# A second head group's chunk states and state products as float32r triples, with gate columns kept in DRAM and decays computed in place

## The chip, the cores and the metric

The kernel runs on one core of a Trainium2 chip. A time is the device time of one execution in microseconds (us). A core has five instruction streams that run side by side and wait for each other by semaphores: TensorE (PE, matrix products), VectorE (DVE), ScalarE (ACT), GpSimd (POOL) and SyncE (SP, which here only issues DMAs). "PEld" in the profile is PE's loading of the stationary operand, which overlaps its products. POOL issues a few DMAs too.

## The reference

One block of a decoder over 1024 positions of width 1024, all in float32. Two kinds of mixer share one input projection and one output projection; a squared-ReLU MLP follows.

```python
u = rms_norm(h, g_mix) * (1 + scale_m) + shift_m
proj = u @ w_in                                   # columns: pool | z | xBC | dt
y_pool = pool_mixer(proj[pool], w_pool, pool_scale)   # windows 2, 4, 8, 16
y_ssd = ssd_mixer(z, u_xbc, u_dt, ...)
h = h + gate_m * (concat(y_pool, y_ssd) @ w_out)
h = h + gate_f * (relu(u2 @ w_up)**2 @ w_down)        # u2: norm of h again
return rms_norm(h, g_final)
```

The state-space mixer (SSD) has 2 groups of 8 heads, 64 wide, with a state of 128, and goes over 8 chunks of 128 positions. Of it:

```python
scores = einsum('bclgn,bcsgn->bclsg', cc, bc)               # C times B inside a chunk
y_diag = einsum('bclsgr,bcsgrp->bclgrp', scores * decay_in, xdt)
states = einsum('bclgn,bclgr,bclgrp->bcgrpn', bc, decay_out, xdt)    # chunk states
# scan over the chunks: h * dec + st, each chunk gets the state ahead of it
y_off = einsum('bclgn,bcgrpn,bclgr->bclgrp', cc, prev, exp(a_cum))   # C times state
y = (y_diag + y_off + d_skip * xs) * silu(z)
```

The products of a chunk's B with the decayed inputs (chunk states) and of its C with the running state are the ones that the change touches; and, of `silu(z)`, the first 240 of the 1024 gate columns.

## The kernel before

Large products run as three float32r products of high and low parts (`mm3`): a float32 operand is cast to float32r on ACT (the high part), DVE subtracts that from the operand (the low part), and PE adds high × high, high × low and low × high in one PSUM bank. Each is a row of line 247 in the profile. The small products of the SSD are plain float32 matmuls. They are shown as two records each (x2, "passes").

The program runs in this order:

1. Startup, then projections for x, B and C of head group 0, with the causal convolution behind each (to about 245 us, with group 1's projections in their second half). Among them, `z0_tok` computes the first 240 gate columns and the dt columns for each of 8 row tiles: ACT takes tanh into `zt` (2 buffers), and DVE writes the sum into `z0s`, a tile of 128x8x240 that stays in SBUF until the SSD of group 0 multiplies it into `tok`.
2. `queue_ssd(g)` puts 9 items in the list `side`: item c calls `ssd_a(c)` (scores; decays: ACT takes exp of a row `R` into `dec`, DVE multiplies by the scores; `ssd_x` makes `xdt` on DVE and `xw` on POOL; B is turned and copied to `btok`), then `ssd_r(c+1)` (loads the next `R` from `cum_d` and masks it on POOL), then `ssd_b(c-1)`. In `ssd_b`, PE forms C × state into bank `po` (line 743), the 8 products of the decayed scores with `xdt` into `py` (L746), and `btok` × `xw` into `pst_` (L750). POOL then multiplies the state by the chunk's decay (L756), DVE adds `pst_` (L757), adds `py` to `tok` (L758), scales `po` (L761) and adds that (L763).
3. `step()` sits between projections and takes items from `side`. Group 0's items run between group 1's projections (to about 230 us); group 1's run in the pool mixer's stage, one per half of a window group (`pool_half`, L797 to L823, about 240 to 300 us, with `pp` the difference that PE multiplies by `wp` at L821), and the last three between the first 512 gate columns' tiles t = 0, 1, 2 in `z_tok` (300 to 318 us).
4. At t = ZC (3) the pool `mx`, which held all SSD tiles, is closed; its space goes to the pools `late` and `fslots`. `gm` and `gf` (512 KB each, L958 and L959) are loaded there, ada columns are computed on DVE from weights in the ring `raw` of 4 buffers (`ada_chunk`, `acc`, L852 for the first and L854 for the rest), and `z_weights` (L917) loads the second half of the gate weights through the same ring. The ring also serves reloads of `ypool_d` and, by `unit` (L193 to L199), the output projection's weights.
5. Output projection, then the MLP, to the end at 1150 us.

The order on each engine is that of a scheduler which lays the program out ahead of time; tiles with fewer buffers than uses make a writer wait for the readers of the buffer's last use. `rows of SP` below are DMAs in the order in which the one queue takes them: one that waits holds back all behind it.

Of the kernel before, what the change touches and what calls it, by code (L numbers as in the profile page):

```python
# [27 lines left out]
HD = 64  # L28
# [22 lines left out]
Z0 = 240  # L51
# [21 lines left out]
def tile_hybrid_block(  # L73
# [24 lines left out]
    pe, act, dve, pool, sp = nc.tensor, nc.scalar, nc.vector, nc.gpsimd, nc.sync  # L98
# [141 lines left out]
    def mm3(ps, whi, wlo, a, first, last, weights_first=True, more=False):  # L240
        ahi, alo = a
        if weights_first:
            three = ((whi, ahi), (whi, alo), (wlo, ahi))
        else:
            three = ((ahi, whi), (ahi, wlo), (alo, whi))
        for i, (st_, mv) in enumerate(three):
            pe.matmul(ps, lhsT=st_, rhs=mv, start=first and i == 0, stop=last and i == 2, skip_group_check=more)  # L247
# [293 lines left out]
    mx = ExitStack()  # L541
    mp = enter(mx, name="mix", bufs=1)
    carry = {ct: mp.tile([P, 4], F32, name=f"carry{ct}") for _, ct in G0}
    z0s = mp.tile([P, NT, Z0], F32, name="z0s")
    dtr = mp.tile([P, NT, HEADS], F32, name="dtr")
    da = mp.tile([P, NT, HEADS], F32, name="da")
    ncum = mp.tile([P, P], F32, name="ncum")
# [4 lines left out]
    BC = {}  # L552
# [42 lines left out]
    def z0_tok(t, ks):  # L595
        ps = bank()
        tok_mm(ps[:, :256], t, ks)
        dve.tensor_tensor(out=dtr[:, t, :], in0=ps[:, Z0:256], in1=dtb, op=ALU.add)
        th = accp.tile([P, 272], F32, name="zt", tag="zt", bufs=2)
        act.activation(out=th[:, :Z0], in_=ps[:, :Z0], func=AF.Tanh, scale=0.5)  # L600
        dve.scalar_tensor_tensor(out=z0s[:, t, :], in0=th[:, :Z0], scalar=1.0, in1=ps[:, :Z0],
                                 op0=ALU.add, op1=ALU.mult)

    def feat(ks, h):
        ps = bank()
# [31 lines left out]
    conv_half(G1[0][1], 1, feat(ks1, 1))  # L637
    step(5.2)

    ax, e_, s_, cumt = (mp.tile([P, HW], F32, name="dec", tag="dec", bufs=4)[:, :P] for _ in range(4))  # L640
    xf = dtr.rearrange("p t h -> p (t h)")
    daf = da.rearrange("p t h -> p (t h)")
    tc.keep_in_program_order(act.activation(out=nea, in_=nea, func=AF.Exp))
# [43 lines left out]

    def ssd_r(g, c_):
        a = c_ * HEADS + g * 8
        R = mp.tile([P, 8, P], F32, name="R", tag="R", bufs=2)  # L690
        sp.dma_start(out=R.rearrange("p h l -> p (h l)"),
                     in_=cum_d[a // 8:a // 8 + 1, :].broadcast_to([P, S]))
        pool.affine_select(out=R, in_=R, pattern=[[0, 8], [1, P]], compare_op=ALU.is_ge, fill=-1e38, base=0,
                           channel_multiplier=-1)
        Rs[(g, c_)] = R

# [14 lines left out]
    def ssd_a(g, c_):  # L711
        B, C = BC[8 + g], BC[10 + g]
        cs = slice(c_ * P, (c_ + 1) * P)
        pscore = bank()
        pe.matmul(pscore[:, :P], lhsT=B[:, cs], rhs=C[:, cs], start=True, stop=True)
        sc = pscore[:, :P]
        Ms = []
        R = Rs.pop((g, c_))
        for b in range(2):
            dec = mp.tile([P, HW], F32, name="dec", tag="dec", bufs=4)  # L720
            dv = dec.rearrange("p (h l) -> p h l", l=P)
            for i in range(4):
                a = c_ * HEADS + g * 8 + b * 4 + i
                act.activation(out=dv[:, i, :], in_=R[:, 4 * b + i, :], func=AF.Exp, bias=ncum[:, a:a + 1])
            dve.tensor_tensor(out=dv, in0=dv, in1=sc.unsqueeze(1).broadcast_to([P, 4, P]), op=ALU.mult)
            Ms.append(dec)
        xdt, xw = ssd_x(g, c_)
        btok = None
        if c_ < NT - 1:
            pb = bank()  # L730
            turn(pb[:, :P], B[:, cs])
            btok = mp.tile([P, P], F32, name="btok", tag="btok", bufs=2)
            act.copy(btok, pb[:, :P])
        live[(g, c_)] = (Ms, xdt, xw, btok)

    def ssd_b(g, c_):
        Ms, xdt, xw, btok = live.pop((g, c_))
        C = BC[10 + g]
        cs = slice(c_ * P, (c_ + 1) * P)
        yv = tok[:, c_, g * 512:(g + 1) * 512]  # L740
        if c_ > 0:
            po = bank()
            pe.matmul(po, lhsT=C[:, cs], rhs=states[g], start=True, stop=True)  # L743
        py = bank()
        for hh in range(8):
            pe.matmul(py[:, hh * HD:(hh + 1) * HD], lhsT=Ms[hh // 4][:, (hh % 4) * P:(hh % 4 + 1) * P],  # L746
                      rhs=xdt[:, hh * HD:(hh + 1) * HD], start=True, stop=True)
        if c_ < NT - 1:
            pst_ = bank()
            pe.matmul(pst_, lhsT=btok, rhs=xw, start=True, stop=True)  # L750
            if c_ == 0:
                states[g] = mp.tile([P, HW], F32, name="state", tag="state", bufs=1)
                act.copy(states[g], pst_)
            else:
                sv = states[g].rearrange("p (h d) -> p h d", d=HD)
                pool.tensor_tensor(out=sv, in0=sv, in1=hbc(cdec, c_, g, HD), op=ALU.mult)  # L756
                dve.tensor_tensor(out=states[g], in0=states[g], in1=pst_, op=ALU.add)  # L757
        dve.tensor_tensor(out=yv, in0=yv, in1=py, op=ALU.add)  # L758
        if c_ > 0:
            y1 = mp.tile([P, HW], F32, name="y1", tag="y1", bufs=1)  # L760
            dve.tensor_tensor(out=y1.rearrange("p (h d) -> p h d", d=HD),  # L761
                              in0=po.rearrange("p (h d) -> p h d", d=HD), in1=hbc(ea, c_, g, HD), op=ALU.mult)
            dve.tensor_tensor(out=yv, in0=yv, in1=y1, op=ALU.add)  # L763
        if g == 0:
            dve.scalar_tensor_tensor(out=tok[:, c_, 0:Z0], in0=tok[:, c_, 0:Z0], scalar=0.5, in1=z0s[:, c_, :],
                                     op0=ALU.mult, op1=ALU.mult)

    def queue_ssd(g):
        ssd_r(g, 0)
        for c_ in range(NT):  # L770
            def one(c_=c_):
                ssd_a(g, c_)
                if c_ + 1 < NT:
                    ssd_r(g, c_ + 1)
                if c_ > 0:
# [776 lines left out]
    for p in range(7):  # L1552
# [6 lines left out]
        ps = sets[key]  # L1559
# [78 lines left out]
```

## Time and profile before

| what | us |
|---|---|
| runs, median of 3 | 1150.16 (1148.13 to 1151.42) |
| profiled execution, its own time | 1152.16 |
| span of the profile | 1150.5 |
| PE busy | 1138.3 (99%) |
| DVE busy | 822.2 (71%) |
| ACT busy | 562.6 (49%) |
| POOL busy | 148.2 (13%) |
| L743, C × state, in 247 to 320 us | 14 records, 7.2 |
| L750, chunk states, there | 14 records, 7.5 |

The granted PE clock was 0.997 of full speed. Busy time is a sum over the span and says little about a stage; the chain that ended last, followed back from the last instruction, says what set the end in each. In the rows of the trace the first number is the start in us from the span's beginning, the second the length; a bracket at the end holds the time that the engine stood idle before it, and what it waited for.

### The profile page before, as it was taken

What the parts mean: (1) busy time and instruction counts of PE and PEld (TensorE: products, weight loads), DVE (VectorE), ACT (ScalarE), POOL (GpSimd) and SP (SyncE); (2) the same over time, 40 slices, a digit from 0 to 9 for tenths busy, and PEclk for the clock granted to TensorE, in tenths of its full rate; (3) what the DMA queues carried; (4) which work ended last, traced back from release to release, by engine and by line L of the source; (5) the groups of instructions that cost most, each with busy time, mean ns of one, the idle gap of its engine ahead of it and who ended that gap; (6) DMA issues with size and microseconds to landing.
All of it is one profiled execution on the core that took longest, in us unless ns stands there. A gap on an engine that the chain in (4) does not pass through costs nothing.

```text
span 1150.5 us, 15234 instructions
## 1 busy us (share of the span) xinstructions
PE 1138.3 (99%) x5541; PEld 948.1 (82%) x5541; DVE 822.2 (71%) x1230; ACT 562.6 (49%) x985; POOL 148.2 (13%) x188
## 2 busy tenths in 40 slices
PE   9999999999999999999999999999999999999997
PEld 9889887877898888888788888888888888888886
DVE  4769989967878667666987666665458744586985
ACT  4477575544354424545774444444434344434373
POOL 3011335425400012022000000000100000000030
PEclk9999999999999999999999999999999999999999
DMA  9932432223256656863165434342599835775832
GB/s 280 254 114 64 131 92 83 93 86 115 74 183 188 226 191 229 257 198 114 36 238 192 174 134 168 143 160 88 211 382 345 308 94 162 254 238 196 279 116 90
DMA packets 123899, 200.72 MB, mean 174 GB/s; under 512 B 8464, under 2 KB 65584, under 8 KB 121776
## 3 DMA queue, kind: packets, MB, share of 16 engines
q1 hardware_dynamic: 122464, 196.24, 50.9%
q0 software_dynamic: 1120, 3.21, 0.9%
q8 instruction: 43, 0.70, 0.3%
q10 hardware_dynamic: 240, 0.30, 0.1%
q14 instruction: 32, 0.26, 0.1%
HBM read 159.81 MB, written 39.91 MB: 174 GB/s over the span
## 4 chain that ended last, share of the span: by engine, by line
PE 79%; DVE 7%; DMA 7%; ACT 2%; issue 2%; POOL 1%; POOLq 0%; SPq 0%; DVEq 0%; ACTq 0%
PE bank L247 70%; DMA raw<-in_w_ada_dram 4%; PE bank L746 2%; DVE acc L854 2%; DMA raw<-ypool_d 1%; DMA raw<-in_w_out_dram 1%; DVE lo L199 1%; PE bank L141 1%; PE bank L750 1%; PE bank L338 1%; PE bank L743 1%; PE bank L821 1%; POOL rst L183 1%; POOL tok L1001 0%; DVE wx L1179 0%
## 5 line engine op out<-in xcount | busy, mean ns | idle before, releaser
L247 PE MATMUL bank<-u,hi 128*128 128x512 f32 x560 | 182.6, 405 | 0.5 <-ACT u L390 0.4
L247 PE MATMUL bank<-dlo,dhi 128*128 128x512 f32 (+1 forms) x464 | 177.2, 382 | 0.0
L247 PE MATMUL bank<-dhi 128*128 128x512 f32 (+1 forms) x464 | 177.2, 382 | 0.0
L247 PE MATMUL bank<-dhi,dlo 128*128 128x512 f32 (+1 forms) x464 | 177.1, 382 | 0.0
L1457 ACT CAST dhi<-fr 128x1024 fp32r<-128x1024 f32 x56 | 58.9, 1052 | 142.8 <-PE bank L247 109.1
L247 PEld LDWEIGHTS bank<-u,hi 128*128 128x128 f32 x560 | 103.7, 189 | 26.6 <-issue 4.8
L1458 DVE TENSOR_TENSOR dlo<-fr,dhi 128x1024 fp32r<-128x1024 f32 x56 | 68.4, 1222 | 78.6 <-ACT dhi L1457 77.9
L247 PE MATMUL bank<-hi,ym 128*128 128x512 f32 x384 | 123.6, 395 | 0.0
L247 PE MATMUL bank<-u,lo 128*128 128x512 f32 x280 | 110.2, 393 | 0.0
L198 ACT CAST hi<-raw 128x512 fp32r<-128x512 f32 (+2 forms) x101 | 62.9, 634 | 80.2 <-DMA raw<-in_w_out_dram 41.6
L247 PEld LDWEIGHTS bank<-dlo,dhi 128*128 128x128 f32 x464 | 87.2, 188 | 17.0
L247 PEld LDWEIGHTS bank<-dhi,dlo 128*128 128x128 f32 x464 | 87.2, 188 | 17.0
L247 PEld LDWEIGHTS bank<-dhi 128*128 128x128 f32 x464 | 87.2, 188 | 16.8
L199 DVE TENSOR_TENSOR lo<-raw,hi 128x512 fp32r<-128x512 f32 (+2 forms) x101 | 75.1, 752 | 30.3 <-ACT hi L198 29.9
L247 PE MATMUL bank<-E,whl 128*128 128x512 f32 x384 | 92.7, 391 | 0.1
L247 PEld LDWEIGHTS bank<-E,whl 128*128 128x128 f32 x384 | 71.7, 188 | 16.6 <-DVE whl L1231 0.9
L247 PEld LDWEIGHTS bank<-hi,ym 128*128 128x128 f32 x384 | 72.1, 188 | 14.8 <-ACT hi L198 0.2
L183 POOL TENSOR_TENSOR rst<-ssq,mhalf 128x1 f32<-128x1 f32 (+2 forms) x27 | 26.5, 984 | 401.7 <-DVE ssq L182 368.2
L247 PE MATMUL bank<-u,whl 128*128 128x512 f32 x312 | 75.6, 389 | 0.0
L247 PE MATMUL bank<-lo,ym 128*128 128x512 f32 x192 | 74.9, 390 | 0.2 <-DVE lo L199 0.2
L247 PEld LDWEIGHTS bank<-u,whl 128*128 128x128 f32 x312 | 58.5, 188 | 12.5 <-DVE whl L1231 0.5
L1231 DVE TENSOR_TENSOR whl<-wraw,whl 128x512 fp32r<-128x512 f32 x58 | 39.9, 688 | 38.4 <-ACT whl L1226 38.3
(272 smaller groups left out, 2144.9 us busy)
## 6 DMA issues: line engine op xcount, KB each, us to landing
f_d<-tok SPq DMA_DIRECT2D x16, 1792.0 KB, 7.1
wr<-in_w_down_dram SPq DMA_DIRECT2D x56, 512.0 KB, 5.6
fr<-f_d SPq DMA_DIRECT2D x53, 512.0 KB, 4.8
raw<-in_w_ada_dram SPq DMA_DIRECT2D x64, 256.0 KB, 2.9
wraw<-in_w_up_dram SPq DMA_DIRECT2D x15, 1024.0 KB, 5.3
raw<-in_w_in_dram SPq DMA_DIRECT2D x48, 256.0 KB, 3.1
raw<-in_w_out_dram SPq DMA_DIRECT2D x48, 256.0 KB, 3.1
tok<-in_x_dram SPq DMA_DIRECT2D x16, 512.0 KB, 6.4
```

Source lines behind the costliest of these rows:

```text
L141: return pe.transpose(dst, src, ident)
L183: pool.tensor_tensor(out=rst[:, a:b], in0=m, in1=mhalf[:, :b - a], op=ALU.pow)
L198: act.copy(hi[:, :n], raw[:, :n])
L199: dve.tensor_tensor(out=lo[:, :n], in0=raw[:, :n], in1=hi[:, :n].bitcast(F32), op=ALU.subtract)
L247: pe.matmul(ps, lhsT=st_, rhs=mv, start=first and i == 0, stop=last and i == 2, skip_group_check=more)
L338: pe.matmul(warm_ps[:, 0:P], lhsT=ones, rhs=ones, start=True, stop=True)
L743: pe.matmul(po, lhsT=C[:, cs], rhs=states[g], start=True, stop=True)
L746: pe.matmul(py[:, hh * HD:(hh + 1) * HD], lhsT=Ms[hh // 4][:, (hh % 4) * P:(hh % 4 + 1) * P], rhs=xdt[:, hh * HD:(hh + 1) * HD], start=Tru ...
L854: dve.scalar_tensor_tensor(out=acc[0], in0=raw, scalar=cact[:, k:k + 1], in1=acc[0], op0=ALU.mult, op1=ALU.add)
L1231: dve.tensor_tensor(out=t_[:, 1], in0=src, in1=t_[:, 0].bitcast(F32), op=ALU.subtract)
L1457: act.copy(hi, src)
L1458: dve.tensor_tensor(out=lo, in0=src, in1=hi.bitcast(F32), op=ALU.subtract)
```

## The change

It has three parts.

For head group 1 only, the chunk-state product and C × state become `mm3` triples. For that, `two_parts` makes high and low parts of the state (`shl`), of `xw` (`xhl`), of `btok` (`bhl`) and of the chunk's C (`chl`), each by a cast on ACT and a subtraction on DVE. Group 0 keeps its float32 matmuls.

The gate columns no longer stay in SBUF: the sum is made in `zt`, stored to `z0_d` by a DMA on POOL's queue (120 KB a tile), and loaded again by SP into a tile `z0` of two buffers, one item ahead of its use.

Decays are computed in place: ACT writes exp over `R`, DVE multiplies there, and the 8 products read it. The tag `dec` with its 4 buffers is gone, `R` has 3 buffers and not 2, and the scratch tiles of the dt block lie in one of them.

```diff
@@ z0_tok
-        dve.scalar_tensor_tensor(out=z0s[:, t, :], in0=th[:, :Z0], scalar=1.0, in1=ps[:, :Z0],
+        dve.scalar_tensor_tensor(out=th[:, :Z0], in0=th[:, :Z0], scalar=1.0, in1=ps[:, :Z0],
                                  op0=ALU.add, op1=ALU.mult)
+        pool.dma_start(out=z0_d[t], in_=th[:, :Z0])
@@ dt block
-    ax, e_, s_, cumt = (mp.tile([P, HW], F32, name="dec", tag="dec", bufs=4)[:, :P] for _ in range(4))
+    dts = mp.tile([P, 8, P], F32, name="R", tag="R", bufs=3)
+    ax, e_, s_, cumt = (dts[:, i, :] for i in range(4))
@@ ssd_r
-        R = mp.tile([P, 8, P], F32, name="R", tag="R", bufs=2)
+        R = mp.tile([P, 8, P], F32, name="R", tag="R", bufs=3)
@@ ssd_a
-            dec = mp.tile([P, HW], F32, name="dec", tag="dec", bufs=4)
-            dv = dec.rearrange("p (h l) -> p h l", l=P)
+            dv = R[:, 4 * b:4 * b + 4, :]
...
-                act.activation(out=dv[:, i, :], in_=R[:, 4 * b + i, :], func=AF.Exp, bias=ncum[:, a:a + 1])
+                act.activation(out=dv[:, i, :], in_=dv[:, i, :], func=AF.Exp, bias=ncum[:, a:a + 1])
...
-            Ms.append(dec)
+            Ms += [dv[:, i, :] for i in range(4)]
@@ new
+    def low_part(v, src):
+        dve.tensor_tensor(out=v[:, 1, :], in0=src, in1=v[:, 0, :].bitcast(F32), op=ALU.subtract)
+
+    def two_parts(name, src, n=HW):
+        v = mp.tile([P, 2, n], F32R, name=name, tag=name, bufs=1)
+        act.copy(v[:, 0, :], src)
+        low_part(v, src)
+        return v
@@ ssd_b
-            pe.matmul(po, lhsT=C[:, cs], rhs=states[g], start=True, stop=True)
+            if g == 0:
+                pe.matmul(po, lhsT=BC[10][:, c_ * P:(c_ + 1) * P], rhs=states[g], start=True, stop=True)
+            else:
+                shl, chl = shls[g], chls.pop((g, c_))
+                mm3(po, shl[:, 0, :], shl[:, 1, :], (chl[:, 0, :], chl[:, 1, :]), True, True, False)
...
-            pe.matmul(pst_, lhsT=btok, rhs=xw, start=True, stop=True)
+            if g == 0:
+                pe.matmul(pst_, lhsT=btok, rhs=xw, start=True, stop=True)
+            else:
+                xp, bp = xhl.pop((g, c_))
+                mm3(pst_, xp[:, 0, :], xp[:, 1, :], (bp[:, 0, :], bp[:, 1, :]), True, True, False)
...
+            if g:
+                shls[g] = two_parts("shl", states[g])
...
-            dve.scalar_tensor_tensor(out=tok[:, c_, 0:Z0], in0=tok[:, c_, 0:Z0], scalar=0.5, in1=z0s[:, c_, :],
+            dve.scalar_tensor_tensor(out=tok[:, c_, 0:Z0], in0=tok[:, c_, 0:Z0], scalar=0.5, in1=z0r.pop(c_),
                                      op0=ALU.mult, op1=ALU.mult)
@@ queue_ssd, in an item
+                if g == 0:
+                    z0r[c_] = mp.tile([P, Z0], F32, name="z0", tag="z0", bufs=2)
+                    sp.dma_start(out=z0r[c_], in_=z0_d[c_])
                 if c_ > 0:
                     ssd_b(g, c_ - 1)
+                if g and c_ < NT - 1:
+                    xhl[(g, c_)] = two_parts("xhl", live[(g, c_)][2]), two_parts("bhl", live[(g, c_)][3], P)
+                if g and c_ > 0:
+                    chls[(g, c_)] = two_parts("chl", BC[10 + g][:, c_ * P:(c_ + 1) * P], P)
```

The changed file's lines are shifted against those of the profile: L743 and L750 of before stand at L248 (`mm3`, L247 before), L746 at L762, L757 at L777, L758 at L780, L761 at L783, L763 at L785, L725 at L730, L852 at L881, L917 at L946, L958 and L959 at L987 and L988.

In the pool stage the triples stand where the float32 matmuls stood. On PE in the z stage, at the item that runs after tile t = 0, before:

```order
L715 MATMUL bank<-ct,bt 128x128
L141 MATMUL bank<-ident,bt 128x128
L743 MATMUL bank<-state,ct 128x512
L746 MATMUL bank<-xdt,dec 128x64 x8
L750 MATMUL bank<-xw,btok 128x512
L247 MATMUL bank<-hi,u 128x272
```

and now, where `hi,u` and `lo,u` are the products of the next tile's gate columns:

```order
L248 MATMUL bank<-shl,chl 128x512
L762 MATMUL bank<-xdt,R 128x64 x8
L248 MATMUL bank<-shl,chl 128x512
L248 MATMUL bank<-xhl,bhl 128x512
...
L248 MATMUL bank<-xhl,bhl 128x512
L248 MATMUL bank<-lo,u 128x272
...
L248 MATMUL bank<-xhl,bhl 128x512
L248 MATMUL bank<-shl,chl 128x512
L248 MATMUL bank<-hi,u 128x272 x2
```

The scheduler took the triples apart: the second product of C × state stands behind the eight products with the decays, and the third one and two of the chunk state's among the next tile's products.

On DVE the first ada product (`acc`) stood in the pool stage, behind the step's last sum, before:

```order
L701 TENSOR_TENSOR xdt<-tok,dt 128x512
L763 TENSOR_TENSOR tok<-tok,y_2953 128x512
L852 TENSOR_SCALAR acc<-raw,cact 128x512
L804 TENSOR_TENSOR psum<-craw 128x527
L725 TENSOR_TENSOR dec<-dec,bank 128x512
```

and stands in the last step of the z stage now, with the low parts in the steps before it:

```order
L777 TENSOR_TENSOR state<-state,bank 128x512
L780 TENSOR_TENSOR tok<-tok,bank 128x512
L783 TENSOR_TENSOR y_3408<-bank,ea 128x512
L742 TENSOR_TENSOR shl<-state,shl 128x512
L785 TENSOR_TENSOR tok<-tok,y_3408 128x512
L742 TENSOR_TENSOR chl<-ct,chl 128x128
...
L939 SCALAR_TENSOR_TENSOR tok<-tok,zt 128x272
L783 TENSOR_TENSOR y_3459<-bank,ea 128x512
L881 TENSOR_SCALAR acc<-raw,cact 128x512
L785 TENSOR_TENSOR tok<-tok,y_3459 128x512
```

The low part of the state is the third operation after the state's sum, and `acc` has moved by about three steps, to right ahead of the last sum of the SSD.

On SP's queue at the same place, before:

```order
L917 DMA raw<-in_w_in_dram 128x512
L816 DMA wp<-in_w_pool_dram 128x128
L823 DMA ypool_d<-yo 128x512
L691 DMA R<-cum_d 128x1024
L823 DMA ypool_d<-yo 128x512 x2
L958 DMA gm<-in_b_ada_dram 128x1024
L959 DMA gf<-in_b_ada_dram 128x1024
```

and now:

```order
L852 DMA ypool_d<-yo 128x512
L946 DMA raw<-in_w_in_dram 128x512
L987 DMA gm<-in_b_ada_dram 128x1024
L988 DMA gf<-in_b_ada_dram 128x1024
L875 DMA raw<-in_w_ada_dram 128x512
L946 DMA raw<-in_w_in_dram 128x512 x2
```

The fourth load of z weights, which takes the buffer that `acc` frees, has moved from ahead of the last pool-stage loads to right ahead of `gm` and `gf`.

More of the change, by code (lines that the diff above doesn't have):

```diff
@@ L133, in tile_hybrid_block @@
     ypool_d = dramp.tile([4, P, S], F32, name="ypool_d")
+    z0_d = [dramp.tile([P, Z0], F32, name=f"z0_d{t}") for t in range(NT)]
     hres_d = [dramp.tile([P, D], F32, name=f"hres{t}") for t in range(NT)]
@@ L543, in tile_hybrid_block @@
     carry = {ct: mp.tile([P, 4], F32, name=f"carry{ct}") for _, ct in G0}
-    z0s = mp.tile([P, NT, Z0], F32, name="z0s")
     dtr = mp.tile([P, NT, HEADS], F32, name="dtr")
@@ L680, in tile_hybrid_block @@
     states = {}
+    shls = {}
+    z0r = {}
+    xhl = {}
+    chls = {}
     def hbc(t, c_, g, n):
@@ L734, in ssd_a @@
         live[(g, c_)] = (Ms, xdt, xw, btok)
+    def low_part(v, src):
[5 more added lines that the diff above has]
+        return v
     def ssd_b(g, c_):
         Ms, xdt, xw, btok = live.pop((g, c_))
-        C = BC[10 + g]
-        cs = slice(c_ * P, (c_ + 1) * P)
         yv = tok[:, c_, g * 512:(g + 1) * 512]
@@ L742, in ssd_b @@
             po = bank()
-            pe.matmul(po, lhsT=C[:, cs], rhs=states[g], start=True, stop=True)
+            if g == 0:
[3 more added lines that the diff above has]
+                mm3(po, shl[:, 0, :], shl[:, 1, :], (chl[:, 0, :], chl[:, 1, :]), True, True, False)
         py = bank()
         for hh in range(8):
-            pe.matmul(py[:, hh * HD:(hh + 1) * HD], lhsT=Ms[hh // 4][:, (hh % 4) * P:(hh % 4 + 1) * P],
+            pe.matmul(py[:, hh * HD:(hh + 1) * HD], lhsT=Ms[hh],
                       rhs=xdt[:, hh * HD:(hh + 1) * HD], start=True, stop=True)
```

## The prediction

> **What bounds the kernel now.** I read the page's busy shares first, then the chain that ended last, then the waits in the stretch where that chain leaves TensorE (PE).
>
> ```profile
> PE 1138.3 (99%) x5541; PEld 948.1 (82%) x5541; DVE 822.2 (71%) x1230; ACT 562.6 (49%) x985; POOL 148.2 (13%) x188
> ...
> PE 79%; DVE 7%; DMA 7%; ACT 2%; issue 2%; POOL 1%; POOLq 0%; SPq 0%; DVEq 0%; ACTq 0%
> ```
>
> PE is busy for 99% of the span, yet the chain gives it only 79%. The difference lies in one stretch, as the chain's own rows in order of time show:
>
> ```profile
> 301.29 0.86 PE bank L743 x2
> ...
> 303.88 0.91 PE bank L750 x2
> ...
> 317.96 6.04 PE bank L247 x48
> ...
> 329.06 4.11 DMA raw<-in_w_ada_dram
> ...
> 336.87 3.53 DMA raw<-in_w_ada_dram
> ...
> 461.25 6.57 DMA raw<-in_w_out_dram
> ...
> 468.50 0.70 DVE lo L199
> ...
> 469.24 2.79 PE bank L247 x11
> ...
> 586.32 552.85 PE bank L247 x2470
> ```
>
> Up to 324 us (317.96 + 6.04) PE sets the end. From 329 to 469 us the chain runs through loads into the four `raw` buffers, each waiting for VectorE (DVE) or ScalarE (ACT) to free one. PE works there too, but meets that ring just in time, at 469.24. Then PE sets the end again: 2470 matmuls without a gap from 586 us. A microsecond that PE wins before 324 us therefore reaches the end only if the ring also starts a microsecond earlier. All edits lie before 320 us. The second group's stage, 247 to 320 us, cut at its steps:
>
> ```profile
> 263.00:273.00 10.00, 10.00 (x50) 7.75 (x49) 8.49 (x14) 4.66 (x13) 6.62 (x7) 1.00 0.26 88
> ...
> 284.00:294.00 10.00, 10.00 (x50) 7.62 (x50) 8.16 (x15) 3.88 (x11) 5.89 (x5) 1.00 0.27 98
> 294.00:304.00 10.00, 10.00 (x70) 8.53 (x69) 10.00 (x16) 4.82 (x16) 5.12 (x4) 1.00 0.07 26
> 304.00:312.00 8.00, 8.00 (x51) 6.33 (x49) 6.20 (x11) 3.94 (x12) 4.56 (x4) 1.00 0.21 68
> 312.00:320.00 8.00, 8.00 (x61) 7.31 (x60) 5.67 (x11) 2.67 (x6) 0.00 (x0) 1.00 0.29 98
> sum 73.00, PE 73.00 PEld 58.28 DVE 56.78 ACT 31.90 POOL 30.19; mean PE 10.43 PEld 8.33 DVE 8.11 ACT 4.56 POOL 4.31
> ```
>
> The columns are the stretch, its length, then busy time of PE, weight loads, DVE, ACT and POOL. PE is full everywhere. DVE has 16.2 us free over 73, but 1.5 and 1.8 us in a pool step and none from 294 to 304.
>
> **The change part by part.**
>
> *Products.* Seven C×state and seven chunk-state matmuls cost 0.86 and 0.91 us (chain rows above). A float32r triple of that size is what the projections run; the first products of two triples, six triples apart:
>
> ```profile
> 220.64 0.62 PE L247 MATMUL bank<-u,hi 128*128 128x512 f32 x2
> ...
> 224.74 0.62 PE L247 MATMUL bank<-u,hi 128*128 128x512 f32 x2
> ```
>
> 4.10 / 6 = 0.68 us, or 0.23 a product. Saved: 7 × 0.18 + 7 × 0.23 = 2.9 us, taken as it stands, since the same shapes run in both rows. "FP8 and Floating Point Precision" of the Trainium skill (TensorE Precision Notes) says that true FP32 takes four passes; that would be 0.91 us for both kinds and a saving of 14 × 0.23 = 3.2 us. The 0.86 us of the C×state row is a little below it, so I use the rows.
>
> *Splitting the operands.* For each of seven chunks ACT casts and DVE subtracts: state and x·w (512 wide), B and C (128 wide).
>
> ```profile
> 305.50 0.68 DVE L758 TENSOR_TENSOR tok<-tok,bank 128x512 f32<-128x512 f32 x1
> 306.10 0.69 DVE L761 TENSOR_TENSOR y<-bank,ea 128x512 f32<-128x512 f32 x1
> ```
>
> ```profile
> L908 DVE SCALAR_TENSOR_TENSOR zt<-zt,bank 128x272 f32<-128x272 f32 x3 | 1.3, 432 | 1.4 <-ACT zt L907 1.3
> L919 ACT CAST zw<-raw 128x512 fp32r<-128x512 f32 x3 | 1.6, 611 | 0.0
> L733 ACT COPY btok<-bank 128x128 f32<-128x128 f32 x7 | 1.8, 258 | 0.0
> ```
>
> DVE: 14 × 0.60 (the pace of the two rows) + 14 × 0.25 (128 wide; below 0.43 for 272, and 0.60 × 128/512 = 0.15 is the floor) = 11.9 us, 1.7 per step. ACT: 14 × 0.61 + 14 × 0.26 = 12.2 us, against 41 us free: no cost by itself. The state's cast and subtraction lengthen the recurrence: state add, cast, subtraction, product. The state add and the product that needs it:
>
> ```profile
> 304.90 0.69 DVE L757 TENSOR_TENSOR state<-state,bank 128x512 f32<-128x512 f32 x1 [0.73 <-PE bank L750]
> ...
> 308.70 1.02 PE L743 MATMUL bank<-state,ct 128*128 128x512 f32 x2
> ```
>
> From 305.59 to 308.70 there are 3.1 us. The triple's first product needs only the cast: 2.5 us are left. Its later products stand behind eight matmuls. From 294 to 304 DVE has no room for its 1.7 us, so it runs that late: 0.8 us are left. By the order DVE also has `y` ahead of `shl`, and `y` waits for the split triple's last product, some products later. I take 0.7 us of stall for the three steps of the z stage, between 0 and 1.4 (twice).
>
> *The first low part.* At 240 us DVE now has `xhl` between the two short corrections of `pp`, for which PE waits:
>
> ```profile
> 239.42 0.16 DVE L813 TENSOR_TENSOR pp<-pp,craw 128x1 f32<-128x1 f32 x1
> ...
> 240.37 1.02 PE L821 MATMUL bank<-pp,wp 128*128 128x512 f32 x2
> ```
>
> 0.8 us separate them. A subtraction of 0.60 fits; one of 1.5 (below) doesn't, by 0.7. I take 0.3. PE at 320 us is then 2.9 − 0.7 − 0.3 = 1.9 us earlier, between 0.8 and 2.9.
>
> *Gate columns.* Eight 120 KB stores on POOL's queue and eight reloads on SP's. The tanh result stays in one of two `zt` buffers until its store lands, and ACT and what is behind it (weight casts, convolution) waits for that. Nearest rows: the POOL queue's 512 KB loads, and the stretch itself.
>
> ```profile
> fr<-f_d POOLq DMA_DIRECT2D x3, 512.0 KB, 9.2
> ```
>
> ```profile
> 60.00:110.00 50.00, 49.70 (x326) 45.15 (x325) 40.27 (x76) 37.23 (x68) 8.63 (x23) 1.00 0.25 69
> ```
>
> At most 9.2 us for a buffer, at least a quarter of it, 2.3. ACT has 12.8 us free and PE is fed from weights cast ahead; I take 0, with up to 2 us in the range. The issues stand on POOL ahead of the convolution's `craw` and `carry` copies. The reloads have tens of microseconds before their use, behind `cum_d` rows on SP: 0. DVE's work is the same in count.
>
> *Decays in place, three R slots.* No instruction is added. A row of decays no longer waits for a `dec` slot, and its cast of the next chunk can begin earlier; R's next load waits for PE's last use instead of ACT's. With three slots that is two steps back: 0.
>
> *Loads at the end of the stage.* On SP the fourth z-weight load now stands right ahead of `gm` and `gf`, and waits for the first ada product on DVE, which has moved into the z stage. So 1 MB that was issued at 310 us, into idle queues, comes at about 318, ahead of the ring's own loads.
>
> ```profile
> gm<-in_b_ada_dram SPq DMA_DIRECT2D x1, 512.0 KB, 4.2
> ```
>
> Next, z weights can be cast only into space of the closed pool, after the last step's sum:
>
> ```profile
> 318.72 0.69 DVE L763 TENSOR_TENSOR tok<-tok,y 128x512 f32<-128x512 f32 x1
> 319.33 1.89 DVE L920 TENSOR_TENSOR zw<-raw,zw 128x512 fp32r<-128x512 f32 x3
> ```
>
> The last triple's third product stands behind projections, and `acc` (0.5 to 0.7 us) ahead of that sum: about 1.5 us given back of the 1.9. So the ring starts between 1 us earlier and 2 us later (half of the 4.2 us of one bias load). I take 0, and with it the end does not move: PE reaches 469 us earlier and waits there.
>
> *Sum.* Profiled execution: 1152.16 us (span 1150.5), now about 1152.2. That run lies 2.0 us over the median of the runs, 1150.16; against that median the forecast is **1150.2 us**. About 0.3%, 3.4 us, is what a measurement of this kernel can tell from no change.
>
> **The rivals.**
>
> *A: the gain is kept.* The ring starts as much earlier as PE is. For it: its start hangs on the z stage's last step, which PE sets. Against: the moved loads. Gain 1.9 to 2.9 us, so 1147.3 to 1148.3; below 1146.7 only if PE's wait for the subtraction at 468.50 (0.70 us) goes too.
>
> *B, the other side: DVE becomes the bound of the second group's steps.* The added subtractions read two SBUF tiles, and such an operation beside POOL takes more than twice as long here:
>
> ```profile
> 235.74 0.68 DVE L701 TENSOR_TENSOR xdt<-tok,dt 128x512 f32<-128x512 f32 x1
> 236.34 1.53 DVE L808 SCALAR_TENSOR_TENSOR pp<-psum,craw 128x512 f32<-128x512 f32 x1
> 237.79 1.53 DVE L701 TENSOR_TENSOR xdt<-tok,dt 128x512 f32<-128x512 f32 x1
> ```
>
> ```profile
> 235.83 1.49 POOL L705 TENSOR_TENSOR xw<-tok,wdt 128x512 f32<-128x512 f32 x1
> 237.40 1.37 POOL L707 TENSOR_TENSOR tok<-tok,dsk 128x512 f32<-128x512 f32 x1
> ```
>
> POOL is busy for 41% of the stage (30.19 / 73). If all collide, 14 × 0.85 = 11.9 us more, and 23.8 against 16.2 free: 7.6 us that PE must wait, less the 2.9 saved, +4.7 us, 1154.9. With the 41%, 4.9 more and 16.8 against 16.2: about nothing. It decides when a step's DVE work passes its 10 us, that is when more than 1.5 to 1.8 us come in, and 1.7 do. "SBUF — State Buffer" of the Trainium skill (SBUF: two separate sides) calls the port pair of DVE and GpSimd an exclusive lock, taken also by a DVE operation with two SBUF inputs against a GpSimd one that reads SBUF, the other fully blocked. The rows of 1.53 us agree, so this rival keeps a real chance.
>
> *C: the ring starts late.* `gm` and `gf` cost it both landings' overlap, 2 to 4 us: 1152 to 1154.
>
> *D: the triple is no cheaper.* If switching weights between short groups costs the 0.2 us, PE gains nothing and the stalls stay: +0 to +2, 1150 to 1152. Against: 0.68 us is held over six triples with a new weight at each product.
>
> **How the numbers follow.** The forecast (the end moves by −1.5 to +2 us) 0.58; A 0.16; B 0.14; C 0.07; D 0.05. Faster by over 0.3% is A's far end, about half of its chance: 0.08. Slower by over 0.3% is B's and a part of C's, 0.16. The rest, 0.76, is within it. The range goes from A with a gain of 3.4, 1146.8, to near B's price, 1154.4.
>
> **What would show it.** Right: 0.68 us per triple, PE full from 247 to 320 us apart from under 1 us; DVE near full in each step; `gm` issued near 318 us; the chain on `raw` loads from 329 to 469 us and PE's wait near 469 us 1 to 2 us longer. Wrong: PE rows in the pool stage that wait for `pp` or `shl` (B), a first ring row over 2 us later (C), PE's arrival at 469 earlier without a wait (A), or ACT waiting for a `zt` store near 100 us with PE behind it.

## The result, and the profile after

The changed kernel takes 1161.64 us (median of 6 runs, 1159.35 to 1166.56) against 1150.62 for the kernel before (6 runs, 1148.13 to 1152.06): a ratio of 1.0092 with a 95% interval of 1.0071 to 1.0114. It is slower, by about 10.6 us (11.0 between the medians); 1150.2 had been forecast, with 1154.4 as the upper end. The profiled execution took 1164.92 us (span 1163.2) and is thus one of the longer runs; the span was 1157.6 in the shortest.

The busy shares and the chain's shares of the page, after:

```profile
PE 1143.0 (98%) x5555; PEld 954.3 (82%) x5555; DVE 841.4 (72%) x1258; ACT 571.3 (49%) x1013; POOL 156.7 (13%) x196
...
PE 70%; DVE 12%; DMA 8%; ACT 4%; issue 3%; POOL 2%; POOLq 0%; DVEq 0%; ACTq 0%; SPq 0%
```

Nine points of the chain have left PE, five of them to DVE. DVE has 19 us more work in the whole span. The same stretches of the group 1 stage (length, then busy time of PE, weight loads, DVE, ACT, POOL; the PE clock granted is the third number from the end):

```profile
263.00:273.00 10.00, 10.00 (x53) 8.29 (x52) 6.87 (x14) 5.96 (x16) 3.83 (x6) 1.00 0.26 89
273.00:284.00 11.00, 9.94 (x52) 7.94 (x51) 11.00 (x15) 5.85 (x16) 5.24 (x5) 1.00 0.30 95
284.00:294.00 10.00, 8.36 (x37) 6.74 (x36) 10.00 (x15) 4.41 (x13) 6.16 (x5) 0.81 0.27 75
294.00:304.00 10.00, 10.00 (x47) 8.06 (x45) 10.00 (x18) 5.06 (x15) 3.61 (x3) 0.85 0.17 63
304.00:312.00 8.00, 8.00 (x63) 7.69 (x62) 8.00 (x11) 4.50 (x13) 5.28 (x4) 1.00 0.22 68
312.00:320.00 8.00, 7.46 (x50) 6.42 (x49) 8.00 (x16) 3.35 (x8) 2.73 (x3) 1.00 0.04 15
```

From 273 us on DVE has no gap, and PE, full everywhere before, has gaps. (DVE is VectorE, ACT ScalarE and POOL GpSimd; the texts below use the long names too.) The waits of PE from 225 to 330 us (in all, times, longest), of which the kernel before had none:

```profile
PE bank L248 <- DVE chl L742: 2.7, 2, 1.6
PE bank L850 <- DVE pp L842: 1.9, 1, 1.9
PE bank L248 <- ACT shl L746: 1.5, 2, 1.0
```

The longest wait for `chl` on PE's timeline, and what follows it:

```profile
286.62 0.71 PE L248 MATMUL bank<-shl,chl 128*128 128x512 f32 x2
288.97 0.50 PE L248 MATMUL bank<-shl,chl 128*128 128x512 f32 x1 [1.64 <-DVE chl L742]
289.30 2.74 PE L762 MATMUL bank<-xdt,R 128*128 128x64 f32 x16
...
294.08 0.63 PE L248 MATMUL bank<-u,lo 128*128 128x512 f32 x1
294.51 1.05 PE L248 MATMUL bank<-u,hi 128*128 128x512 f32 x2
```

The third product of the triple needs the low part of C, the last of the low parts in VectorE's step. After this wait PE's products take longer: the eight with decays 2.74 us (1.89 in the step at 266.44), and a product of the next tile 0.43 us (294.08 to 294.51) and not 0.23. The granted clock has fallen, to 0.52 from 290 to 295 us (shown in the last section). VectorE is late because its step has become longer than PE's. From the first sum over `craw` in one step to that in the next it works without a gap:

```profile
278.35 1.54 DVE L833 TENSOR_TENSOR psum<-craw 128x527 f32<-128x527 f32 x1
...
290.07 1.54 DVE L833 TENSOR_TENSOR psum<-craw 128x527 f32<-128x527 f32 x1
```

That is 11.72 us, against 9.82 of a step of PE without a wait (shown below), and PE's two waits for `chl`, at 277.25 and 288.97, lie 11.72 us apart too. What fills the step, in VectorE's own operations, start and length:

```profile
284.04 0.68 DVE L742 TENSOR_TENSOR shl<-state,shl 128x512 fp32r<-128x512 f32 x1
284.64 0.68 DVE L783 TENSOR_TENSOR y<-bank,ea 128x512 f32<-128x512 f32 x1
285.24 0.97 DVE L742 TENSOR_TENSOR xhl<-xw,xhl 128x512 fp32r<-128x512 f32 x1
286.14 1.53 DVE L785 TENSOR_TENSOR tok<-tok,y 128x512 f32<-128x512 f32 x1
287.59 1.12 DVE L742 TENSOR_TENSOR bhl<-btok,bhl 128x128 fp32r<-128x128 f32 x1
288.63 0.28 DVE L742 TENSOR_TENSOR chl<-ct,chl 128x128 fp32r<-128x128 f32 x1
```

`bhl` and `chl` are the same operation on the same shape: 1.12 and 0.28 us. Between 285.64 and 288.57 GpSimd multiplies the state and makes `xw`; `bhl` ends just after that, and `chl` runs alone. Over the stage (247 to 330 us; busy, mean ns):

```profile
L742 DVE TENSOR_TENSOR bhl<-btok,bhl 128x128 fp32r<-128x128 f32 x7 | 6.2, 886 | 0.0
L742 DVE TENSOR_TENSOR xhl<-xw,xhl 128x512 fp32r<-128x512 f32 x6 | 6.1, 1014 | 0.0
...
L742 DVE TENSOR_TENSOR shl<-state,shl 128x512 fp32r<-128x512 f32 x7 | 4.8, 681 | 0.5 <-ACT shl L746 0.5
...
L742 DVE TENSOR_TENSOR chl<-ct,chl 128x128 fp32r<-128x128 f32 x6 | 1.7, 278 | 0.0
```

6.2 + 6.1 + 4.8 + 1.7 = 18.8 us. Where PE then stands, from the chain after: the last products with decays, and the long gapless end.

```profile
324.33 1.73 PE bank L762 x16
...
599.34 20.80 PE bank L248 x90
```

316.23 has become 324.33, 8.1 us later; 586.32 has become 599.34, 13.0 us. In this profiled execution 8.1 us were lost in the second group's stage, and 4.9 between 324 and 586 us. Of the 8.1, the waits of 2.7 + 1.9 + 1.5 = 6.1 us and 3.4 us by the lower clock, less 2.3 that the products save (both below), make 7.2. Of the 4.9, PE's idle time from 326 to 586 us makes 2.3 (4.0 and not 1.7), and a second fall of the clock, to 0.66 from 505 to 510 us, 1.7.

### The profile page after: what moved, and what is told of

It reads as the page before. It is cut to its first block, busy times and chain, and to the rows that moved or that the text cites. A ratio compares the mean times of both kernels' runs of the same rounds, so it can differ in the third digit from the quotient of the medians.

```text
span 1163.2 us, 15369 instructions
## 1 busy us (share of the span) xinstructions
PE 1143.0 (98%) x5555; PEld 954.3 (82%) x5555; DVE 841.4 (72%) x1258; ACT 571.3 (49%) x1013; POOL 156.7 (13%) x196
## 4 chain that ended last, share of the span: by engine, by line
PE 70%; DVE 12%; DMA 8%; ACT 4%; issue 3%; POOL 2%; POOLq 0%; DVEq 0%; ACTq 0%; SPq 0%
PE bank L248 63%; DMA raw<-in_w_ada_dram 3%; DMA raw<-in_w_out_dram 2%; PE bank L762 2%; DVE lo L200 2%; DMA raw<-ypool_d 1%; DVE acc L883 1%; PE bank L339 1%; PE bank L142 1%; POOL rst L184 1%; DVE psum L833 1%; ACT tok L956 1%; DMA R<-cum_d 1%; DMA raw<-in_w_in_dram 1%; DVE whl L1260 1%
## 5 line engine op out<-in xcount | busy, mean ns | idle before, releaser
L248 PE MATMUL bank<-u,hi 128*128 128x512 f32 x560 | 182.4, 405 | 0.5 <-ACT u L391 0.4
L248 PE MATMUL bank<-dlo,dhi 128*128 128x512 f32 (+1 forms) x464 | 177.2, 382 | 0.0
L248 PE MATMUL bank<-dhi 128*128 128x512 f32 (+1 forms) x464 | 177.2, 382 | 0.0
L248 PE MATMUL bank<-dhi,dlo 128*128 128x512 f32 (+1 forms) x464 | 177.1, 382 | 0.0
L248 PE MATMUL bank<-hi,ym 128*128 128x512 f32 x384 | 125.4, 399 | 1.7 <-DVE tok L1104 1.1
L248 PEld LDWEIGHTS bank<-u,hi 128*128 128x128 f32 x560 | 104.6, 191 | 25.5 <-issue 3.6
L248 PE MATMUL bank<-u,lo 128*128 128x512 f32 x280 | 110.8, 396 | 0.0
L248 PEld LDWEIGHTS bank<-dhi 128*128 128x128 f32 x464 | 87.2, 188 | 17.2
L248 PEld LDWEIGHTS bank<-dhi,dlo 128*128 128x128 f32 x464 | 87.2, 188 | 16.9
L248 PEld LDWEIGHTS bank<-dlo,dhi 128*128 128x128 f32 x464 | 87.2, 188 | 16.8
L248 PE MATMUL bank<-E,whl 128*128 128x512 f32 x384 | 92.6, 390 | 0.1
L248 PEld LDWEIGHTS bank<-hi,ym 128*128 128x128 f32 x384 | 72.8, 190 | 17.8 <-DVE tok L1104 1.5
L248 PEld LDWEIGHTS bank<-E,whl 128*128 128x128 f32 x384 | 71.6, 188 | 16.5 <-DVE whl L1260 0.9
L248 PE MATMUL bank<-u,whl 128*128 128x512 f32 x312 | 75.6, 390 | 0.1
L248 PE MATMUL bank<-lo,ym 128*128 128x512 f32 x192 | 75.4, 393 | 0.0
L248 PEld LDWEIGHTS bank<-u,whl 128*128 128x128 f32 x312 | 58.5, 188 | 12.6 <-DVE whl L1260 0.5
```

## The experiments

Ratios are against runs of the kernel before on the same chip, with 95% intervals; the changed kernel stands at 1.0092. VectorE's busy time is that of the stretch from 273 to 294 us of the profiled run, 21.00 being all of it (before: 17.03). It does not order the ratios: e14 is full and loses next to nothing; e6 and e8 are not, because VectorE idled 3.7 us for `craw` there, and lose as much as the others.

| kernel | ratio | interval | VectorE |
|---|---|---|---|
| e15: gate columns alone | 0.9996 | 0.9986 to 1.0005 | 17.51 |
| e1: gate columns, decays in place | 1.0015 | 1.0004 to 1.0027 | 18.19 |
| e5: all, low parts not on VectorE | 1.0010 | 0.9997 to 1.0023 | 20.90 |
| e14: chunk states, decays apart | 1.0006 | 0.9993 to 1.0018 | 21.00 |
| e2: chunk states, decays in place | 1.0053 | 1.0036 to 1.0069 | 20.55 |
| e13: C × state, decays apart | 1.0029 | 1.0017 to 1.0042 | 21.00 |
| e3: C × state, decays in place | 1.0053 | 1.0034 to 1.0071 | 21.00 |
| e7: parts made, not used | 1.0064 | 1.0044 to 1.0084 | 21.00 |
| e17: e16 and B from PSUM | 1.0072 | 1.0056 to 1.0088 | 21.00 |
| e4: all, B from PSUM | 1.0080 | 1.0068 to 1.0092 | 21.00 |
| e8: all, bias loads elsewhere | 1.0080 | 1.0061 to 1.0100 | 17.37 |
| e6: all, less GpSimd work | 1.0081 | 1.0061 to 1.0101 | 18.14 |
| e9: all, pool stores elsewhere | 1.0089 | 1.0071 to 1.0106 | 21.00 |
| e16: all, exps in order | 1.0094 | 1.0077 to 1.0112 | 21.00 |

**Which part (e1, e2, e3).** The edits take a triple back to one float32 matmul, and its parts with it:

```diff
-                mm3(po, shl[:, 0, :], shl[:, 1, :], (chl[:, 0, :], chl[:, 1, :]), True, True, False)
+            pe.matmul(po, lhsT=BC[10 + g][:, c_ * P:(c_ + 1) * P], rhs=states[g], start=True, stop=True)   # e1, e2
-                mm3(pst_, xp[:, 0, :], xp[:, 1, :], (bp[:, 0, :], bp[:, 1, :]), True, True, False)
+            pe.matmul(pst_, lhsT=btok, rhs=xw, start=True, stop=True)                                     # e1, e3
```

> The changed kernel with group 1's two products back in float32; gate columns through DRAM and decays in place stay. Theory T1 (VectorE is overfull: each step of group 1 lasts as long as its VectorE work, low parts and their collisions with GpSimd included): no low parts, so near the kernel before, 1149 to 1152 us, steps of about 10.15 us again. Theory T2 (the products are innocent; the later R loads, the exps ahead of the convolution's copies and the z0 path make it slow): near the changed kernel, 1157 to 1162 us, with VectorE waiting in the steps.

> Only the chunk-state product as a triple (low parts of xw and B: in the changed kernel 1014 and 886 ns each, 13 us of VectorE in seven steps); C times state in float32. T1: a step's VectorE work is about 8.5 + 1.9 = 10.4 us against 10.0 us of PE: most of the loss remains or a third to two thirds of it, 1153 to 1159 us. T2: like e1, whatever that is, within 2 us.

> Only C times state as a triple (low parts of the state and of C: 681 and 278 ns each, 6.7 us of VectorE in seven steps). T1: 8.5 + 1.0 = 9.5 us of VectorE in a step of 10.0: it fits, 1149 to 1152 us, and VectorE has idle time in the pool stage. T2: like e1 within 2 us. A third theory, T3 (the low part of C is the last VectorE operation of a step, and PE waits for it, whatever the load): PE waits for chl of 1 us or more stay here and it is slower than e1 by 3 us or more.

e1 took 1154.11 us (2 us above T1's range), a ratio of 1.0015: most of the loss comes with the triples and what belongs to them. Each half alone is at 1.0053, e2 within T1's range. For e3 T1 expected no loss, since 1.0 us of VectorE's time seemed to fit a step; it did not: VectorE is full from 273 to 294 us there as well. e3 is 3.6 us above e1, as T3 said, but the wait for `chl` that T3 gave as the reason is absent; PE waits for `shl` (1.1 us) and twice at a product with `pp` (0.8 and 1.7) there.

**Is it the products or VectorE's work (e5, e7)?** e5 keeps every product and makes the low parts by copies on ScalarE, so that they hold the whole operand and the values of group 1 are other ones; e7 makes all parts and reads none.

```diff
 # e5, in low_part
-        dve.tensor_tensor(out=v[:, 1, :], in0=src, in1=v[:, 0, :].bitcast(F32), op=ALU.subtract)
+        act.copy(v[:, 1, :], src)
```

> The changed kernel with the four low parts of group 1 made by copies on ScalarE in place of subtractions on VectorE (the low parts hold the whole operand, so the values of group 1 are other ones; all products and waits between engines stay). VectorE loses 28 operations, about 18.5 us in the group 1 stage; ScalarE gains about 12. T1 (VectorE's load): the loss is gone and some of the 2.9 us that PE saves may show, 1147 to 1152 us, PE without waits from 247 to 320 us. T4 (the recurrence is longer: state, cast, low part, product, whatever the load): it stays as long, so PE still waits in each step and the time stays above 1155 us.

> The kernel e1 (group 1's products in float32) with all high and low parts made as in the changed kernel, but read by nobody. T1: VectorE has the load of the changed kernel, PE has 2.9 us more, so 1157 to 1163 us, with PE waiting for float32 operands that VectorE makes late (state, decays, pp). T4: no product waits for a part, so like e1, 1151 to 1154 us.

e5: 1153.68 us against 1153.23, ratio 1.0010. With all triples in place and 28 VectorE operations fewer the loss is gone. The stage in e5:

```profile
273.00:294.00 21.00, 20.53 (x105) 16.38 (x103) 20.90 (x29) 14.02 (x39) 10.27 (x11) 1.00 0.36 115
294.00:320.00 26.00, 25.00 (x180) 23.15 (x181) 22.04 (x38) 18.25 (x52) 8.75 (x8) 1.00 0.15 54
```

VectorE gets out of its backlog after 294 us (22.04 of 26). PE was not free of waits, as T1 had said: it waited 1.8 and 1.4 us at products with `pp`. e7: 1.0064, with the products of e1 and the load of the changed kernel; PE waits for the state's sum there:

```profile
PE bank L755 <- DVE state L769: 2.2, 2, 1.8
PE bank L842 <- issue: 2.1, 1, 2.1
PE bank L842 <- DVE pp L834: 1.3, 1, 1.3
```

So, with decays in place, VectorE's added operations suffice for most of the loss, and without them the loss is gone. That the longer recurrence (T4) costs nothing is not shown to the last microsecond: e5 should then gain the 2.3 us of the products over e1, and the two intervals overlap too far to tell.

**Collisions with GpSimd (e4, e6).** e4 takes B's parts straight from the turned B in PSUM; e6 leaves out GpSimd's multiplication by `d_skip` in group 1.

```diff
 # e4, in ssd_a, for group 1
-            btok = mp.tile([P, P], F32, name="btok", tag="btok", bufs=2)
-            act.copy(btok, pb[:, :P])
+            btok = two_parts("bhl", pb[:, :P], P)
```

> The changed kernel, with B's high and low parts in group 1 taken from the turned B in PSUM and no copy of it in SBUF: the subtraction reads one SBUF tile and not two. T1 with collisions: that subtraction falls from 886 ns to about 280, 4.2 us less VectorE over seven steps, and the time falls by about 4 us, to 1156 to 1159 us. T1 without collisions (the 886 ns come from something else): it stays near 886 ns and the time near 1161. T2: near 1161 too, though the subtraction is short. T3: near 1161, PE still waits for chl.

> The changed kernel without GpSimd's multiplication by d_skip in group 1 (eight operations of 1.0 to 1.4 us beside VectorE; the skip term of group 1 is then not scaled). VectorE has the same instructions. T1 with collisions: each GpSimd operation on two SBUF operands costs VectorE up to 0.85 us, the excess over the shortest duration of each form, 10.8 us in the stage, falls by 4 to 6 us, and the time by about the same, 1155 to 1158 us. If collisions only fill time that VectorE would wait anyway: 1159 to 1162.

In e4 (247 to 325 us):

```profile
L745 DVE TENSOR_TENSOR xhl<-xw,xhl 128x512 fp32r<-128x512 f32 x6 | 7.0, 1168 | 0.0
L707 DVE TENSOR_TENSOR xdt<-tok,dt 128x512 f32<-128x512 f32 x6 | 6.6, 1106 | 0.0
...
L745 DVE TENSOR_TENSOR chl<-ct,chl 128x128 fp32r<-128x128 f32 x6 | 3.4, 560 | 0.0
L745 DVE TENSOR_TENSOR bhl<-bank,bhl 128x128 fp32r<-128x128 f32 x7 | 1.9, 277 | 0.0
```

The subtraction from PSUM takes 277 ns and not 886, as T1 with collisions said. But `xhl` went from 1014 to 1168, `chl` from 278 to 560 and `xdt` from 678 to 1106: GpSimd's operations now meet other ones. The time followed little, 1161.24 us, 1.0080 against 1.0092, with intervals that overlap. e6, which does not scale the skip term of group 1, took 1161.57 us, 1.0081, where T1 with collisions expected 1155 to 1158; the other side of the expectation, 1159 to 1162, came in. `xhl` fell to 921 ns and `bhl` to 764, but VectorE waited for `craw` (3.7 us, to 275.86), ran late after that, and PE waited 3.4 us for `chl`. That operations are stretched is shown; that removing stretches gives the time back is not.

**The loads of gm and gf (e8).**

```diff
-                sp.dma_start(out=gm, in_=b_ada[:, 2 * D:3 * D].broadcast_to([P, D]))
+                act.dma_start(out=gm, in_=b_ada[:, 2 * D:3 * D].broadcast_to([P, D]))   # and gf
```

> The changed kernel with the loads of gm and gf issued by ScalarE's queue, no longer ahead of the ada and z-weight loads on SP's. If the 1 MB held the ring up (rival C): 1 to 4 us faster, 1157 to 1160 us. If PE's lateness before 325 us is what counts: within 1 us of the changed kernel, 1160.6 to 1162.6.

1161.52 us, 1.0080, against 1.0092 for the change: rival C has no visible part in it, though the intervals would leave room for a microsecond or two. (As in e6, VectorE idled before 277 us in this profile, and PE waited 3.4 us for `chl`.)

**A loop through the decay rows (e9, e10, e11, e12).** In the changed kernel VectorE idles 3.1 us ahead of its sum over `craw` at 267.03: the copy of `craw` stands behind exps on ScalarE that wait for a row `R`. The four kernels store the pool mixer's output from ScalarE's queue: the changed kernel (e9), e1 (e10), e4 (e11) and before (e12).

```diff
-            sp.dma_start(out=ypool_d[gi, :, h * HW:(h + 1) * HW], in_=yo)
+            act.dma_start(out=ypool_d[gi, :, h * HW:(h + 1) * HW], in_=yo)
```

> The changed kernel with the stores of the pool mixer's output issued by ScalarE's queue, behind the activation that makes them, so that on SP's queue the load of the next decay row R no longer stands behind a store that waits for PE's product with pp. Theory T5 (a loop across engines: pp's product, its store, the R load behind it on SP, GpSimd's select, the exps on ScalarE, the copy of craw behind them, VectorE's sums, pp again; VectorE's new work lengthens the last part beyond the 10.15 us step): the loop is cut, the waits of 3 to 4 us for craw on VectorE go, and the time falls by 4 us or more, to a ratio of 1.005 or less. T1 (VectorE's work alone is longer than the step): it stays full, a ratio of 1.007 to 1.009.

> The kernel e1 (float32 products in group 1) with the same stores on ScalarE's queue. T5: what e1 loses against before (0.15%) goes, ratio 0.998 to 1.000. T1: no change to e1, 1.000 to 1.003.

> The kernel e4 (B's parts taken from PSUM, so one subtraction of two SBUF tiles fewer in a step) with the same stores on ScalarE's queue. T5: like e9 or 1 to 2 us faster than it, ratio 0.999 to 1.004; if VectorE then fits the step, the 2.9 us of the triples show and it beats the kernel before. T1: like e4, 1.007 to 1.009.

> Control: the kernel before with the same stores on ScalarE's queue. It has VectorE time to spare in each step and no PE wait in the stage, so all theories expect no change, ratio 0.998 to 1.002.

1.0089, 1.0015 (1.0002 to 1.0028), 1.0096 (1.0076 to 1.0117) and 1.0001 (0.9989 to 1.0014): nothing moved. The store is not all that a load of `R` waits for: with decays in place it takes a slot that PE's products with decays must have read. For that it waited 7.0 us in all from 225 to 330 us in the changed kernel, and 17.8 in e9. In the kernel before these loads waited for ScalarE's exps (`dec`). The wait for `craw` stayed too (e9):

```profile
266.27 0.82 DVE L833 TENSOR_TENSOR psum<-craw 128x527 f32<-128x527 f32 x1 [4.39 <-ACT craw L829]
```

**Decays in place or apart (e13, e14, e15).** A half triple leaves room in SBUF for the old tiles.

```diff
-            dv = R[:, 4 * b:4 * b + 4, :]
+            dec = mp.tile([P, HW], F32, name="dec", tag="dec", bufs=4)
+            dv = dec.rearrange("p (h l) -> p h l", l=P)
```

> The kernel e3 (only C times state as a triple; it was at a ratio of 1.0053) with decays in tiles of their own again (dec with 4 buffers, R with 2), so the exps of a chunk stand a chunk later on ScalarE. T5 (VectorE's work added to a loop that runs through the early exps): the waits for craw go and the loss with them, ratio 0.998 to 1.002. T1 (VectorE's load alone): 1.004 to 1.007.

> The kernel e2 (only chunk states as triples; 1.0053) with decays in tiles of their own again. T5: 0.998 to 1.003. T1: 1.004 to 1.007.

> The kernel before with only the gate columns kept in DRAM (float32 products, decays in tiles of their own). e1 (this with decays in place) was at 1.0015. T5: the in-place decays made that small loss, so 0.999 to 1.001 here. T1, or the stores on GpSimd's queue: the loss of e1 stays, 1.001 to 1.003.

With decays apart the chunk states cost 1.0006 and not 1.0053 (intervals apart), C × state 1.0029 and not 1.0053 (intervals overlap), no triple 0.9996 and not 1.0015 (they just overlap). So the in-place decays have a share in the loss, together with VectorE's work; T5's numbers came in for e14 and e15, half for e13. In place the halves add up: 0.0053 + 0.0053 − 0.0015 = 0.0091, and the whole is at 0.0092. If they add up with decays apart too, the whole change would be at 0.0006 + 0.0029 + 0.0004 = 0.0039 there, less than half of the loss. That is an estimate; the whole change with decays apart was not run. VectorE is full from 273 to 294 us in e13 and e14 as well, and gets out of it later (24.48 and 22.57 of 26 us from 294 to 320; e3 25.50, e2 24.36).

**Only the place of the exps (e16, e17).** The whole change, exps of group 1 held behind craw and `yo` on ScalarE; e17 with B from PSUM.

```diff
-                act.activation(out=dv[:, i, :], in_=dv[:, i, :], func=AF.Exp, bias=ncum[:, a:a + 1])
+                ex = act.activation(out=dv[:, i, :], in_=dv[:, i, :], func=AF.Exp, bias=ncum[:, a:a + 1])
+                if g:
+                    tc.keep_in_program_order(ex)
```

> The whole change, but with group 1's exps kept in the order of the program on ScalarE: the eight exps of a chunk stand behind the copy of craw and behind yo of their half, not two chunks ahead of need in front of craw. VectorE's instructions are the same. T5 (the early exps hold craw, and through it VectorE, pp and PE): most of the loss goes, ratio 0.999 to 1.004, and VectorE's waits for craw of 3 to 4 us on ScalarE's exps are gone. T1 (VectorE's load alone): 1.007 to 1.010. In between (1.005 to 1.007): both.

> e16 with B's parts taken from PSUM (as in e4: the subtraction reads one SBUF tile). T5: like e16 or up to 0.002 below it, the best candidate for a version as fast as before, 0.997 to 1.003. T1: 1.006 to 1.009, like e4.

1.0094 and 1.0072: T5 falls for the whole change. With the exps in order VectorE is just as full and PE waits for the same tiles (e16):

```profile
273.00:294.00 21.00, 17.60 (x86) 14.09 (x85) 21.00 (x30) 10.18 (x30) 8.04 (x8) 0.92 0.36 115
294.00:320.00 26.00, 23.26 (x149) 20.30 (x148) 25.32 (x43) 13.10 (x38) 11.23 (x10) 1.00 0.12 43
...
PE bank L248 <- DVE chl L744: 3.9, 3, 2.4
PE bank L248 <- ACT shl L748: 2.3, 2, 1.6
```

**What stays open.** By which waits the in-place decays add to the halves is known in part. One stands at the start of the stage, in the changed kernel:

```profile
235.36 1.28 ACT L729 ACTIVATE R<-R,ncum 128x128 f32<-128x128 f32 x4 [1.78 <-POOL R L699]
236.55 0.57 ACT L829 COPY craw<-bank 128x512 f32<-128x512 f32 x1
...
242.32 1.10 PE L850 MATMUL bank<-pp,wp 128*128 128x512 f32 x2 [1.86 <-DVE pp L842]
```

Four exps, computed early, wait for GpSimd's select of `R`, and the copy of `craw` stands behind them (it began at 234.20 before, as soon as PE was done). VectorE's sums and `pp` follow it, and PE waits. This wait is 0.8 us in e1 and e3, 1.2 in e2 and 1.8 in e5, all with decays in place; it is absent in e13 and e15, with decays apart, and 0.3 in e16 and e17, with the exps in order. It is not the whole: e16 loses as much as the change, with 3.9 us of waits for `chl`. What remains is not explained by the store ahead of R's load (e9) or the place of the exps (e16). None of the versions beats the kernel before; e15 and e14 cannot be told from it.

## Why the prediction was wrong

*The bound.* Right as far as it went: PE sets the end up to 324 us, and what it loses there comes out at the end.

*Products.* The mechanism was right, the size not quite. A step without a wait, from one product with `pp` to the next, before and after:

```profile
272.82 1.02 PE L821 MATMUL bank<-pp,wp 128*128 128x512 f32 x2
282.97 1.02 PE L821 MATMUL bank<-pp,wp 128*128 128x512 f32 x2
```

```profile
264.56 1.02 PE L850 MATMUL bank<-pp,wp 128*128 128x512 f32 x2
...
274.38 1.02 PE L850 MATMUL bank<-pp,wp 128*128 128x512 f32 x2
```

10.15 against 9.82 us: a pair of triples saves 0.33 us, where 0.41 was expected, 2.3 and not 2.9 us in seven steps. The two steps hold the same products otherwise. Rival D falls.

*Splitting the operands: the step that failed.* 11.9 us had been put for VectorE, by undisturbed paces; the four groups measured 18.8. The operations that had been there took about as long as before in sum (63.0 us, 63.2 before): `tok` at L785 went from 682 to 1043 ns, but `xdt` from 797 to 678. The 0.7 us of stall taken for it came out as waits of 2.7 us for `chl` and 1.5 for `shl`, plus the loss by the clock. It had been put into the three steps of the z stage; the waits for `chl` stand in the pool stage, and PE, which was to be 1.9 us earlier at the end of the stage, was 8.1 later. Two errors of reasoning stand behind the size. VectorE's free time was added up over the stage, 16.2 us, although 8.1 of it lay ahead of 273 us (17.88 busy of 26 from 247) and was not used: after the change VectorE still idles there (17.57 of 26), for `craw` above all, and has no gap from 273 on. And only `shl` was followed to its reader; the low part of C, last in VectorE's step, was not, though PE's third product waits for it.

*The first low part* at 0.3: the wait for `pp` at 242 us was 1.86. `xhl` between the two corrections took 0.6 of it (241.42 to 242.03), as the prediction's rows said it would; the rest came from the late copy of `craw` (236.55 against 234.20), which the prediction did not have.

*Rival B* named the mechanism and the side, with a chance of 0.14 and 1154.9 us. Its rule (a step's VectorE work against its 10 us) was the right one: 1.7 us by undisturbed paces against 1.5 to 1.8 free was already no margin, and 18.8 / 7 = 2.7 us is well past it. Its price was short not in VectorE's work (23.8 us if all collide; 18.8 came) but in the free time set against it, 16.2 us, of which only the 8.1 behind 273 us were filled; the lower clock after waits comes on top. "SBUF — State Buffer" of the Trainium skill (SBUF: two separate sides), which the prediction cited for it, agrees with what was measured here: 277 ns from PSUM, 886 ns from SBUF.

*Gate columns* at 0: right (e15, 0.9996). *Decays in place* at 0: the second step that failed. That exps can begin earlier was counted as harmless, but they hold up the copy of `craw` at the start of the stage. It costs about 0.002 alone (e1 against e15) and 0.005 with the chunk states (e2 against e14). *Loads at the end of the stage*, and rival C: no part that shows (e8), although `gm` was issued only at 328.90 us and not near 318. *Rival A*: PE was never earlier, so it could not show.

## What to carry to other kernels

Before work is moved to an engine that is off the critical path, price it in the steps where it must be done, with the durations of the rows that run beside a neighbour, and follow each new result to its reader; free time ahead of the work is no cover. An engine at 85% of a step is full when a sixth is added. A faster product that needs prepared operands is paid by whoever prepares them: here 2.3 us of PE cost 18.8 of VectorE.

## What the runs showed of the hardware

PE's granted clock fell after short waits. After the wait of 1.64 us at 288.97 (and one of 1.06 at 277.25):

```profile
285.00:290.00 5.00, 3.36 (x18) 2.29 (x18) 5.00 (x7) 3.95 (x12) 3.90 (x4) 1.00 0.05 13
290.00:295.00 5.00, 5.00 (x19) 4.32 (x19) 5.00 (x8) 1.15 (x3) 1.68 (x2) 0.52 0.60 181
295.00:300.00 5.00, 5.00 (x19) 4.03 (x18) 5.00 (x9) 2.16 (x7) 2.46 (x3) 0.80 0.07 29
```

5 × 0.48 + 5 × 0.20 = 3.4 us of PE's time. "TensorE: Matmul & The Clock Gate" of the Trainium skill (HAM oscillation) warns of idle gaps of more than about 3.4 us. Here less was enough. But the wait of 1.86 us at 242.32 in the same execution was followed by no drop, nor were those of 1.7 us in e3, 1.9 in e17 and 2.2 in e7, so the length of the wait alone does not decide. Nor does it set the price. Added up over slices of 2 us from 240 to 340, a fall costs 1.7 us in e2, e9 and e16, after waits of 1.9, 1.4 and 2.4, and 3.4 us in the changed kernel, e4 and e8, after 1.6, 1.6 and 3.4; the lowest slice of these is 0.50 but in e9, where two of 0.56 and 0.59 share the fall.

The spread of the changed kernel's runs goes with the clock: spans of 1157.6, 1157.8, 1159.7, 1160.1, 1163.2 and 1164.9 us have mean clocks of 0.997, 0.996, 0.995, 0.995, 0.992 and 0.990, and 0.007 of 1160 us is 8 us. Only the run of 1163.2 has a trace here, so this is no more than a match. The loss does not need it: the shortest run, at the 0.997 of the kernel before in its profile, is still 7.1 us longer than that (1157.6 against 1150.5).

And a stretched operation is not tied to its place: freed of one meeting, GpSimd's operation stretches a later VectorE operation that reads two SBUF tiles (e4: `chl` 278 to 560 ns, `xdt` 678 to 1106).
